# Second feed-forward product: blocks P3 and P7 exchanged, the last norms spread over P7 and P4 without GpSimd

## The chip, the cores and the metric

One core of one Trainium2 chip runs the whole layer in float32. The metric is the device time of one execution in microseconds (us). Three runs of the kernel before gave 1181.56, 1182.09 and 1875.72 us; the median is 1182.09 us. The profiled execution took 1181.23 us, with a span of 1179.4 us from its first to its last instruction.

## The reference

The layer is a mixer (convolution, chunkwise mLSTM, differential attention, an output product), a norm, a feed-forward part and a second norm. Only the end matters here:

```python
x = layer_norm(DEEPNORM_ALPHA * x + h, ln1_g[l], ln1_b[l])
h = jnp.square(jax.nn.relu(x @ w_up[l])) @ w_down[l]
x = layer_norm(DEEPNORM_ALPHA * x + h, ln2_g[l], ln2_b[l])
```

x is 1024 x 1024, w_up 1024 x 4096, w_down 4096 x 1024. `layer_norm` subtracts the mean of each token's 1024 values, divides by the root of the variance plus 1e-5, multiplies by g and adds b.

## The kernel before

The second feed-forward product (hidden 1024 x 4096 by w_down 4096 x 1024) is computed with seven block products instead of eight (Strassen's scheme), P1 to P7. Tokens stand in eight tiles ("rows" 0 to 7, 128 tokens each), output columns in two halves of 512. Every operand is split into a rounded part `hi` (a cast on ACT) and a rest `lo` (a subtraction on DVE), so each product is three matmuls: hi hi, lo hi, hi lo.

The product runs in two passes (c = 0 and 1, half of the hidden units each), a pass in seven blocks of GC = 4 steps, a step in 24 matmuls of 128x512. One table sets the order of the blocks; the table of the first product, `ORDER`, serves both. `down_prep(n)` loads the hidden tile of step n (`hraw`), casts and subtracts; it is called AHEAD = 3 steps early. The weight block of step n is B11, B21, B22 or a sum T1 to T4. Tiles live in 47 slots that are handed out in the order in which they were given back.

A block accumulates in four PSUM banks, one for a token tile: P1, P6, P7, P4 in one set (`abank`), P2, P5, P3 in the other (`bbank`); P1, P2 and P5 start on new banks, the others add on top of what stands there. After a block `gather` adds its banks to the accumulators `accs[row]` on DVE, one instruction of 128x512 for each bank. So P1, P2 feed columns 0 of rows 0 to 3, P6 and P3 their columns 1, P5 and P7 columns 1 of rows 4 to 7, P4 their columns 0. Rows 0 to 3 are complete after P3, rows 4 to 7 after P4. In the second pass P4 runs row by row (4 x 24 matmuls), and the norm of a row follows its gather.

`last_norm` takes statistics with two BN_STATS of 512 columns and one BN_AGGR on DVE, the inverse root as Ln and Exp on ACT with one Newton step on DVE, and applies them one row later: columns 0 on ACT (scale and bias), then DVE (gain) and GpSimd (bias), columns 1 in two DVE instructions. Row 6 has its gain on GpSimd too; row 7 runs on DVE alone, its output in four pieces. All transfers are issued on SP's queue.

The instructions of an engine stand in the order in which a scheduler put them by priority when the program was built; an engine works them off in that order, and one that waits holds up those behind it.

Of the kernel before, what the change touches and what calls it, by code (L numbers as in the profile page):

```python
# [31 lines left out]
EPS = 1e-5  # L32
# [65 lines left out]
def mixer_block(ctx: ExitStack, tc: tile.TileContext, a: dict, out: bass.AP):  # L98
    nc = tc.nc
    const = ctx.enter_context(tc.tile_pool(name="const", bufs=1))  # L100
    spool = ctx.enter_context(tc.tile_pool(name="slots", bufs=1))
    small = ctx.enter_context(tc.tile_pool(name="small", bufs=2))
# [6 lines left out]
    act, dve = nc.scalar, nc.vector  # L109
# [7 lines left out]
    def load(out, in_):  # L117
        nc.sync.dma_start(out=out, in_=in_)
# [19 lines left out]
    epsc = const.tile([P, 1], F32, name="epsc")  # L138
# [32 lines left out]
    css = [slice(half * 512, half * 512 + 512) for half in range(2)]  # L171
# [619 lines left out]
        load(b[:, :D], a[name + "_b"].to_broadcast([P, D]))  # L791
        return g, b

    def stats(z, full=True, n=2):

        st = small.tile([P, n, 6], F32, tag=f"bst{n}", name="bst", bufs=4 // n)
        for i in range(n):
            dve.bn_stats(out=st[:, i, :], in_=z[:, i * (D // n):(i + 1) * (D // n)])  # L798
        mv = small.tile([P, 5], F32, name="bmv")
        dve.bn_aggr(out=mv[:, 0:2], in_=st)  # L800
        act.activation(mv[:, 2:3], mv[:, 1:2], AF.Ln, bias=epsc)
        act.activation(mv[:, 2:3], mv[:, 2:3], AF.Exp, scale=-0.5)

        dve.tensor_scalar(out=mv[:, 1:2], in0=mv[:, 1:2], scalar1=EPS, scalar2=None, op0=ALU.add)
        dve.scalar_tensor_tensor(out=mv[:, 3:4], in0=mv[:, 2:3], scalar=mv[:, 1:2],
                                 in1=mv[:, 2:3], op0=ALU.mult, op1=ALU.mult)
        dve.scalar_tensor_tensor(out=mv[:, 2:3], in0=mv[:, 3:4], scalar=3.0, in1=mv[:, 2:3],  # L807
                                 op0=ALU.subtract, op1=ALU.mult)
        if full:
            dve.tensor_scalar(out=mv[:, 2:3], in0=mv[:, 2:3], scalar1=-0.5, scalar2=None,  # L810
                              op0=ALU.mult)
        return mv


# [2 lines left out]
    b0, b1, b2 = (ml_qk(b) for b in range(3))  # L817
# [94 lines left out]
    F = Slots(spool, [])  # L912
# [39 lines left out]
    def add(out, p, q):  # L952
        dve.tensor_tensor(out=out, in0=p, in1=q, op=ALU.add)  # L953
# [8 lines left out]
    ORDER = ("P1", "P2", "P6", "P5", "P7", "P3", "P4")  # L962
# [192 lines left out]


    GC = NS // 4
    NSTEP = 2 * 7 * GC
    wd, ops_d = {}, {}

    def wd_load(c, g, names):
        s0 = 2 * (GC * c + g)
        for nme in names:
            i, j = int(nme[1]) - 1, int(nme[2]) - 1
            t = F.alloc(F32, nme)
            load(t[:, :1024].rearrange("p (s n) -> p s n", s=2),
                 a["w_down"][NS * i + s0:NS * i + s0 + 2, :, 512 * j:512 * j + 512]
                 .rearrange("s p n -> p s n"))
            wd[c, g, nme] = t
# [22 lines left out]

    def step_of(n):
        c, r = divmod(n, 7 * GC)
        return c, ORDER[r // GC], r % GC

    def down_prep(n):
        c, p, g = step_of(n)
        n_ = slice(0, 1024)
        raw = F.alloc(F32, "hraw")  # L1200
        load(raw[:, n_].rearrange("p (s n) -> p s n", s=2), hdram[GC * c + g][:, HOF[p], :, :])
        keep = c == 0 and BOF[p] in ("B11", "B21")
        ops_d[n] = (*halves_of(raw),
                    *halves_of(wd[c, g, BOF[p]] if keep else wd.pop((c, g, BOF[p])), keep))
# [17 lines left out]
    accs, seen = {}, set()  # L1222
# [9 lines left out]
    def acc_load(rows):  # L1232
        for tb in rows:
# [3 lines left out]
    TO = dict(P1=((0, 0),), P2=((0, 0),), P6=((0, 1),), P5=((4, 1),), P7=((4, 1),), P3=((0, 1),),  # L1237
              P4=((4, 0),))

    def last_norm(tb):  # L1240

        z = accs[tb][:, :D]
        mv = stats(z, False, 2)
        mu, w = mv[:, 0:1], mv[:, 2:3]

        def apply():
            if tb == TB - 1:
                for cs in css:
                    dve.scalar_tensor_tensor(out=z[:, cs], in0=z[:, cs], scalar=mu, in1=g2[:, cs],
                                             op0=ALU.subtract, op1=ALU.mult)  # L1250
                for i in range(4):
                    cs = slice(i * 256, i * 256 + 256)
                    dve.scalar_tensor_tensor(out=z[:, cs], in0=z[:, cs], scalar=w, in1=b2[:, cs],
                                             op0=ALU.mult, op1=ALU.add)
                    load(out[tb * P:tb * P + P, cs], z[:, cs])
                return
            za, zb = z[:, css[0]], z[:, css[1]]
            dve.scalar_tensor_tensor(out=mv[:, 4:5], in0=mu, scalar=-1.0, in1=w, op0=ALU.mult,
                                     op1=ALU.mult)
            act.activation(za, za, AF.Identity, scale=w, bias=mv[:, 4:5])  # L1260
            dve.scalar_tensor_tensor(out=zb, in0=zb, scalar=mu, in1=g2[:, css[1]],
                                     op0=ALU.subtract, op1=ALU.mult)
            mul = nc.gpsimd if tb == TB - 2 else dve
            mul.tensor_tensor(out=za, in0=za, in1=g2[:, css[0]], op=ALU.mult)
            nc.gpsimd.tensor_tensor(out=za, in0=za, in1=b2[:, css[0]], op=ALU.add)
            dve.scalar_tensor_tensor(out=zb, in0=zb, scalar=w, in1=b2[:, css[1]], op0=ALU.mult,  # L1266
                                     op1=ALU.add)
            load(out[tb * P:tb * P + P, css[1]], zb)
            load(out[tb * P:tb * P + P, css[0]], za)

        late.append(apply)
        while len(late) > (0 if tb == TB - 1 else 1):
            late.popleft()()

    late = deque()


    with lane(6):
# [77 lines left out]
    g2 = b2 = None  # L1356
    for n in range(NSTEP):
        c, p, g = step_of(n)
        k = n % (7 * GC)
        final = c == 1 and p == "P4"  # L1360
        if c == 0 and k < GC:
            wd_load(0, k, ("B12",))
        if c == 0 and 2 <= k < 2 + GC:
            wd_load(0, k - 2, ("B22",))
        if n + AHEAD < NSTEP:
            down_prep(n + AHEAD)
        if g == 0:
            if p in ("P1", "P2", "P5"):
                banks = [bank() for _ in range(4)]
                if p == "P1":  # L1370
                    abank[:] = banks
                else:
                    bbank[:] = banks
        if not final:
            down_mm(n, range(4), g == 0, g == GC - 1)
            F.free(*ops_d.pop(n))
        elif g == GC - 1:
            for tb in range(4):
                for m in range(n - GC + 1, n + 1):
# [123 lines left out]
```

## Time and profile before

| | us |
|---|---|
| median of the runs shown | 1182.09 |
| profiled execution | 1181.23 |
| its span | 1179.4 |
| PE busy in the span | 1135.5 (96%) |
| DVE busy | 848.3 (72%) |
| ACT busy | 558.8 (47%) |
| POOL (GpSimd) busy | 13.8 (1%) |

A row of the timeline shows start, duration, engine, line, operation, output and inputs of an instruction; "x4" merges equal ones that follow each other, and what stands in brackets is idle time before it and what ended it. A row of a table by stretch shows, for each engine, busy time and number of instructions, then the granted TensorE clock (1.00 is 2.4 GHz), the busy share of the DMA engines and GB/s. Each duration is that of one instruction; neighbours on an engine overlap a little.

### The profile page before, as it was taken

To read this page: it belongs to the slowest core of one execution; us is meant where nothing else is said; L and a number is where in the kernel's file an instruction comes from. 1 tells how busy PE (TensorE), PEld (TensorE's weight loads), DVE (VectorE), ACT (ScalarE), POOL (GpSimd) and SP (SyncE) were. 2 spreads that over 40 slices of the span, in tenths; PEclk is the share of its full clock that TensorE was granted. 3 is DMA by queue.
4 is the path that set the end of the run, shared out by engine and by line. 5 is a ranking of instruction groups with operands and counts; after the bars stand their busy time and mean duration, and the time that the engine had idled before them with its cause. 6 is when DMAs were issued, how large, how long until landed. Compare 5 with 4: busy or idle time off the path is not lost.

```text
span 1179.4 us, 14960 instructions
## 1 busy us (share of the span) xinstructions
PE 1135.5 (96%) x5630; PEld 932.5 (79%) x5630; DVE 848.3 (72%) x1263; ACT 558.8 (47%) x902; POOL 13.8 (1%) x12
## 2 busy tenths in 40 slices
PE   8999999999999999599999999999999999999993
PEld 6898778877887777487888888888888888888882
DVE  5999668864765738789976767655589666766758
ACT  6212483475664628457654444544534323344411
POOL 0000000000000000000000000000000000000013
PEclk9999999999999999799999999999999999999997
DMA  7202135445635671521376464544884545343303
GB/s 278 73 10 72 36 107 155 147 138 155 168 101 177 224 202 59 168 90 60 144 246 244 167 234 170 196 143 152 313 329 171 186 178 170 116 143 125 107 30 113
DMA packets 82648, 179.86 MB, mean 152 GB/s; under 512 B 7760, under 2 KB 29328, under 8 KB 82576
## 3 DMA queue, kind: packets, MB, share of 16 engines
q1 hardware_dynamic: 82576, 178.91, 45.2%
q8 instruction: 44, 0.72, 0.2%
q14 instruction: 28, 0.23, 0.1%
HBM read 120.12 MB, written 58.72 MB: 152 GB/s over the span
## 4 chain that ended last, share of the span: by engine, by line
PE 88%; DVE 6%; DMA 2%; ACT 2%; issue 1%; SPq 0%; DVEq 0%; ACTq 0%
PE f L933 50%; PE mm L112 27%; PE s L112 5%; PE t L112 4%; PE t L115 2%; DMA raw<-in_w_out 1%; DVE bst L798 1%; DVE lo L148 1%; ACT pp L736 1%; DMA vh<-v 0%; DVE bmv L807 0%; DVE nm L734 0%; DVE acc L953 0%; DMA v<-vh 0%; DVE acc L1266 0%
## 5 line engine op out<-in xcount | busy, mean ns | idle before, releaser
L933 PE MATMUL f<-hi,lo 128*128 128x512 f32 x832 | 327.2, 393 | 0.0
L933 PE MATMUL f<-hi 128*128 128x512 f32 x832 | 327.1, 393 | 0.0
L933 PE MATMUL f<-lo,hi 128*128 128x512 f32 x832 | 326.9, 393 | 0.0
L933 PEld LDWEIGHTS f<-hi 128*128 128x128 f32 x832 | 156.6, 188 | 35.7
L933 PEld LDWEIGHTS f<-lo,hi 128*128 128x128 f32 x832 | 156.4, 188 | 35.9
L933 PEld LDWEIGHTS f<-hi,lo 128*128 128x128 f32 x832 | 156.1, 188 | 36.0
L112 PE MATMUL mm<-xh,hi 128*128 128x512 f32 x240 | 95.7, 400 | 5.7 <-ACT xh L147 5.7
L147 ACT CAST hi<-hraw 128x1024 fp32r<-128x1024 f32 x56 | 58.4, 1049 | 89.8 <-DMA hraw<-h 87.6
L148 DVE TENSOR_TENSOR lo<-hraw,hi 128x1024 fp32r<-128x1024 f32 x56 | 68.2, 1222 | 42.7 <-ACT hi L147 39.2
L112 PE MATMUL mm<-xh,lo 128*128 128x512 f32 x240 | 95.9, 400 | 0.0
L112 PE MATMUL mm<-xl,hi 128*128 128x512 f32 x240 | 95.9, 400 | 0.0
L285 DVE SCALAR_TENSOR_TENSOR cacc<-ypad,pc,cacc 128x1024 f32<-128x1024 f32 x60 | 74.2, 1286 | 0.6
L112 PE MATMUL mm<-hi,xh 128*128 128x256 f32 (+1 forms) x256 | 74.0, 289 | 0.0
L112 PE MATMUL mm<-hi,xl 128*128 128x256 f32 (+1 forms) x256 | 73.2, 286 | 0.0
L112 PE MATMUL mm<-lo,xh 128*128 128x256 f32 (+1 forms) x256 | 73.1, 286 | 0.0
L112 PE MATMUL mm<-hi,yh 128*128 128x512 f32 x128 | 52.7, 411 | 10.8 <-ACT yh L147 9.2
L147 ACT CAST hi<-B 128x1024 fp32r<-128x1024 f32 x36 | 37.6, 1049 | 52.0 <-PE f L933 39.3
L736 ACT ACTIVATE pp<-s,nm 128x128 f32<-128x128 f32 (+7 forms) x64 | 47.7, 747 | 27.2 <-DVE nm L734 18.1
L734 DVE TENSOR_REDUCE nm<-s 128x1 f32<-128x128 f32 (+7 forms) x64 | 47.9, 752 | 16.8 <-PE s L112 16.3
L148 DVE TENSOR_TENSOR lo<-B,hi 128x1024 fp32r<-128x1024 f32 x36 | 43.8, 1221 | 18.7 <-ACT hi L147 13.1
L112 PEld LDWEIGHTS mm<-xh,hi 128*128 128x128 f32 x240 | 45.6, 190 | 14.3 <-ACT xh L147 5.7
L148 DVE TENSOR_TENSOR lo<-raw,hi 128x1024 fp32r<-128x1024 f32 (+3 forms) x34 | 39.3, 1161 | 23.4 <-ACT hi L147 19.6
(264 smaller groups left out, 2046.6 us busy)
## 6 DMA issues: line engine op xcount, KB each, us to landing
hraw<-h SPq DMA_DIRECT2D x56, 512.0 KB, 3.5
w<-in_w_up SPq DMA_DIRECT2D x32, 512.0 KB, 5.4
B<-in_w_down SPq DMA_DIRECT2D x32, 512.0 KB, 4.8
h<-hp SPq DMA_DIRECT2D x16, 512.0 KB
h<-hq SPq DMA_DIRECT2D x16, 512.0 KB, 3.1
h<-hx SPq DMA_DIRECT2D x16, 512.0 KB
raw<-in_wfm SPq DMA_DIRECT2D x14, 512.0 KB, 3.8
qk<-th SPq DMA_DIRECT2D x8, 512.0 KB
```

Source lines behind the costliest of these rows:

```text
L112: return nc.tensor.matmul(out, lhsT=lhsT, rhs=rhs, start=start, stop=stop)
L115: nc.tensor.transpose(out, in_, ident[:k, :k])
L147: act.copy(hi, src)
L148: dve.tensor_tensor(out=lo, in0=src, in1=hi.bitcast(F32), op=ALU.subtract)
L285: dve.scalar_tensor_tensor(out=av, in0=yp[:, i:i + S], scalar=col(PC_DWW + 31 * c + i), in1=av, op0=ALU.mult, op1=ALU.add)
L734: dve.tensor_reduce(out=nm[:, m:m + 1], in_=s_[:, 0:nk], axis=AX.X, op=ALU.max, negate=True)
L736: act.activation(pp[m][:, 0:nk], s_[:, 0:nk], AF.Exp, bias=nm[:, m:m + 1], accum_out=sm[:, m:m + 1])
L798: dve.bn_stats(out=st[:, i, :], in_=z[:, i * (D // n):(i + 1) * (D // n)])
L933: return nc.tensor.matmul(out, lhsT=lhsT, rhs=rhs, start=start and not more, stop=stop and not more, skip_group_check=more)
```

## The change

The second product gets an order of its own, in which P3 comes ahead of P7, in both passes. In the second pass the norms of rows 0 to 3 (`first_norm`) stand beside the four steps of P7: their sums are taken on ACT (one pass of Identity and one of Square, each with an accumulator output into a scrap slot `junk`), and scale and bias are applied to all 1024 columns on ACT, gain and bias on DVE. After P7 `half_stats` takes the BN_STATS of columns 1 of rows 4 to 7, ahead of P4. `last_norm` takes only those of columns 0, and finishes each row at once. No instruction is left on GpSimd; rows 0 to 6 leave in one transfer of 128x1024 each instead of two.

```diff
+    ORDER_D = ("P1", "P2", "P6", "P5", "P3", "P7", "P4")
...
-        return c, ORDER[r // GC], r % GC
+        return c, ORDER_D[r // GC], r % GC
...
+    def newton(mv):
+        dve.scalar_tensor_tensor(out=mv[:, 3:4], in0=mv[:, 2:3], scalar=mv[:, 1:2],
+                                 in1=mv[:, 2:3], op0=ALU.mult, op1=ALU.mult)
+        dve.scalar_tensor_tensor(out=mv[:, 2:3], in0=mv[:, 3:4], scalar=3.0, in1=mv[:, 2:3],
+                                 op0=ALU.subtract, op1=ALU.mult)
+
+    def finish_row(tb, mv):
+        z = accs[tb][:, :D]
+        act.activation(z, z, AF.Identity, scale=mv[:, 2:3], bias=mv[:, 4:5])
+        dve.tensor_tensor(out=z, in0=z, in1=g2[:, :D], op=ALU.mult)
+        add(z, z, b2[:, :D])
+        load(out[tb * P:tb * P + P, :], z)
+
+    def first_norm(tb):
+        z = accs[tb][:, :D]
+        junk = F.alloc(F32, "junk")
+        mv = small.tile([P, 6], F32, tag="mvf", name="mvf")
+        act.activation(junk[:, :D], z, AF.Identity, accum_out=mv[:, 0:1])
+        dve.tensor_scalar(out=mv[:, 5:6], in0=mv[:, 0:1], scalar1=-1.0 / D, scalar2=None,
+                          op0=ALU.mult)
+        act.activation(junk[:, :D], z, AF.Square, bias=mv[:, 5:6], accum_out=mv[:, 1:2])
+        act.activation(mv[:, 2:3], mv[:, 1:2], AF.Ln, scale=1.0 / D, bias=epsc)
+        act.activation(mv[:, 2:3], mv[:, 2:3], AF.Exp, scale=-0.5)
+        dve.tensor_scalar(out=mv[:, 1:2], in0=mv[:, 1:2], scalar1=1.0 / D, scalar2=EPS,
+                          op0=ALU.mult, op1=ALU.add)
+        newton(mv)
+        dve.tensor_tensor(out=mv[:, 4:5], in0=mv[:, 5:6], in1=mv[:, 2:3], op=ALU.mult)
+        F.free(junk)
+        finish_row(tb, mv)
...
+    def half_stats(tb):
+        st = halves[tb] = small.tile([P, 2, 6], F32, tag=f"hst{tb}", name="hst", bufs=1)
+        dve.bn_stats(out=st[:, 1, :], in_=accs[tb][:, css[1]])
+
     def last_norm(tb):
-        z = accs[tb][:, :D]
-        mv = stats(z, False, 2)
+        z, st = accs[tb][:, :D], halves[tb]
+        dve.bn_stats(out=st[:, 0, :], in_=z[:, css[0]])
...
+        act.activation(w, mv[:, 1:2], AF.Ln, bias=epsc)
+        act.activation(w, w, AF.Exp, scale=-0.5)
+        dve.tensor_scalar(out=mv[:, 1:2], in0=mv[:, 1:2], scalar1=EPS, scalar2=None, op0=ALU.add)
+        if tb < TB - 1:
+            newton(mv)
...
+            finish_row(tb, mv)
+            return
...
+        if c == 1 and p == "P7":
+            first_norm(g)
...
-            if c == 1 and p == "P3":
-                for tb in range(4):
-                    last_norm(tb)
+            if c == 1 and p == "P7":
+                for tb in range(4, TB):
+                    half_stats(tb)
```

In the rows that follow, `acc_7562`, `acc_7579`, `acc_7606`, `acc_7631` are rows 0 to 3 and `acc_8016`, `acc_8053`, `acc_8090`, `acc_8131` rows 4 to 7; `f_` are PSUM banks, `mvf_` and `bmv_` the small statistics of a row.

On DVE before, this stands from the gathers of P3 in the second pass on:

```order
L953 TENSOR_TENSOR acc_7562<-acc_7562,f_9200 128x512
L953 TENSOR_TENSOR acc_7579<-acc_7579,f_9201 128x512
L798 BN_STATS bst_9614<-acc_7562 128x6
L953 TENSOR_TENSOR acc_7606<-acc_7606,f_9202 128x512
L953 TENSOR_TENSOR acc_7631<-acc_7631,f_9203 128x512
L800 BN_AGGR bmv_9617<-bst_9614 128x2
```

On DVE now, from the end of row 2's norm to the statistics ahead of P4:

```order
L1250 TENSOR_TENSOR acc_7606<-acc_7606,ln2g_9079 128x1024
L1265 TENSOR_SCALAR mvf_9632<-mvf_9632 128x1
L951 TENSOR_TENSOR acc_7606<-acc_7606,ln2b_9080 128x1024
L1241 SCALAR_TENSOR_TENSOR mvf_9632<-mvf_9632 128x1
L1243 SCALAR_TENSOR_TENSOR mvf_9632<-mvf_9632 128x1
L1268 TENSOR_TENSOR mvf_9632<-mvf_9632 128x1
L951 TENSOR_TENSOR acc_8016<-acc_8016,f_8755 128x512
L1250 TENSOR_TENSOR acc_7631<-acc_7631,ln2g_9079 128x1024
L951 TENSOR_TENSOR acc_8053<-acc_8053,f_8756 128x512
L951 TENSOR_TENSOR acc_7631<-acc_7631,ln2b_9080 128x1024
L951 TENSOR_TENSOR acc_8090<-acc_8090,f_8757 128x512
L951 TENSOR_TENSOR acc_8131<-acc_8131,f_8758 128x512
```

The gathers of P7 (banks f_8755 to f_8758, rows 4 to 7) now stand behind the Newton step of row 3 and the whole of rows 0 to 2; the four BN_STATS of columns 1 come right behind them.

At the end of the program DVE had this, from the gather of row 7 on:

```order
L953 TENSOR_TENSOR acc_8131<-acc_8131,f_8758 128x512
L804 TENSOR_SCALAR bmv_9802<-bmv_9802 128x1
L1264 TENSOR_TENSOR acc_8053<-acc_8053,ln2g_9079 128x512
L805 SCALAR_TENSOR_TENSOR bmv_9802<-bmv_9802 128x1
L1266 SCALAR_TENSOR_TENSOR acc_8053<-acc_8053,bmv_9759,ln2b_9080 128x512
L807 SCALAR_TENSOR_TENSOR bmv_9802<-bmv_9802 128x1
L798 BN_STATS bst_9842<-acc_8131 128x6 x2
L1258 SCALAR_TENSOR_TENSOR bmv_9802<-bmv_9802 128x1
L1261 SCALAR_TENSOR_TENSOR acc_8090<-acc_8090,bmv_9802,ln2g_9079 128x512
L800 BN_AGGR bmv_9845<-bst_9842 128x2
```

and has this now:

```order
L1250 TENSOR_TENSOR acc_8090<-acc_8090,ln2g_9079 128x1024
L951 TENSOR_TENSOR acc_8131<-acc_8131,f_8758 128x512
L951 TENSOR_TENSOR acc_8090<-acc_8090,ln2b_9080 128x1024
L1281 BN_STATS hst_9680<-acc_8131 128x6
L1283 BN_AGGR mvf_9832<-hst_9680 128x2
L1295 SCALAR_TENSOR_TENSOR acc_8131<-acc_8131,mvf_9832,ln2g_9079 128x512
L1287 TENSOR_SCALAR mvf_9832<-mvf_9832 128x1
L1295 SCALAR_TENSOR_TENSOR acc_8131<-acc_8131,mvf_9832,ln2g_9079 128x512
```

Between the gather of row 7 and its aggregate there stood parts of rows 5 and 6; now only one addition of row 6 stands there, and the gather itself stands behind row 6's gain.

On PE in the second pass, where P5 ends and P3 begins (banks f_9200 to f_9203 for both), the first matmul on each bank now waits for a semaphore of DVE; the block that followed P5 before wrote other banks:

```order
L931 MATMUL f_9203<-hi_9196,lo_9193 128x512
L931 MATMUL f_9200<-hi_9234,hi_9230 128x512 [waits DVE_49,Activation_49]
L931 MATMUL f_9200<-lo_9235,hi_9230 128x512
L931 MATMUL f_9200<-hi_9234,lo_9231 128x512
L931 MATMUL f_9201<-hi_9234,hi_9230 128x512 [waits DVE_49]
L931 MATMUL f_9201<-lo_9235,hi_9230 128x512
L931 MATMUL f_9201<-hi_9234,lo_9231 128x512
L931 MATMUL f_9202<-hi_9234,hi_9230 128x512 [waits DVE_49]
```

The same holds from P7 to P4, and for both places in the first pass.

## Rows read from the trace of the kernel before

**Rows 1.** First line of the page: the span.

```profile
span 1179.4 us, 14960 instructions
```

**Rows 2.** Busy time by stretch: P7, P3 and P4 of the second pass.

```profile
1114.47:1136.65 22.18, 22.18 (x97) 18.06 (x96) 8.43 (x10) 4.00 (x4) 0.00 (x0) 1.00 0.00 0
1136.65:1158.80 22.15, 22.15 (x97) 17.95 (x96) 22.15 (x52) 5.50 (x14) 6.77 (x4) 1.00 0.19 72
1158.80:1179.40 20.60, 2.15 (x10) 1.40 (x8) 17.59 (x36) 3.83 (x9) 6.84 (x4) 0.61 0.35 127
```

**Rows 3.** Timeline of DVE: gathers of P5, P7 and P3, then the end.

```profile
1092.29 2.78 DVE L953 TENSOR_TENSOR acc<-acc,f 128x512 f32<-128x512 f32 x4
...
1114.47 1.39 DVE L953 TENSOR_TENSOR acc<-acc,f 128x512 f32<-128x512 f32 x2 [0.85 <-PE f L933]
...
1136.65 1.37 DVE L953 TENSOR_TENSOR acc<-acc,f 128x512 f32<-128x512 f32 x2 [12.28 <-PE f L933]
...
1151.59 1.26 DVE L807 SCALAR_TENSOR_TENSOR bmv<-bmv 128x1 f32<-128x1 f32 x1
...
1171.17 1.69 DVE L1249 SCALAR_TENSOR_TENSOR acc<-acc,bmv,ln2g 128x512 f32<-128x512 f32 x1
...
1174.76 1.67 DVE L1253 SCALAR_TENSOR_TENSOR acc<-acc,bmv,ln2b 128x256 f32<-128x256 f32 x4
```

**Rows 4.** Groups of DVE from 1130 us on: busy, mean ns, idle before.

```profile
L798 DVE BATCH_NORM_STATS2 bst<-acc 128x6 f32<-128x512 f32 x14 | 9.1, 672 | 0.0
L807 DVE SCALAR_TENSOR_TENSOR bmv<-bmv 128x1 f32<-128x1 f32 x8 | 5.6, 698 | 0.0
...
L805 DVE SCALAR_TENSOR_TENSOR bmv<-bmv 128x1 f32<-128x1 f32 x8 | 3.0, 380 | 0.0
```

**Rows 5.** Timeline of POOL: one of its eight instructions.

```profile
1151.01 1.83 POOL L1265 TENSOR_TENSOR acc<-acc,ln2b 128x512 f32<-128x512 f32 x1 [2.14 <-issue]
```

**Rows 6.** Groups of ACT over the whole span, columns as before.

```profile
L147 ACT CAST hi<-hraw 128x1024 fp32r<-128x1024 f32 x56 | 58.4, 1049 | 89.8 <-DMA hraw<-h 87.6 <-PE f L933 1.8 <-DVE lo L148 0.3
...
L1128 ACT ACTIVATE hq<-hq 128x1024 f32<-128x1024 f32 x16 | 17.0, 1060 | 0.4
...
L736 ACT ACTIVATION_READ_ACCUMULATOR pp<-s,nm 128x1 f32 x64 | 12.9, 202 | 0.0
...
L903 ACT ACTIVATE acc<-acc,bmv 128x1024 f32<-128x1024 f32 x8 | 9.8, 1242 | 6.0 <-DVE bmv L901 5.9
```

**Rows 7.** Timeline of DVE in the first norm, around one row's aggregate.

```profile
538.40 0.19 DVE L800 BATCH_NORM_AGGREGATE bmv<-bst 128x2 f32<-128x12 f32 x1
```

**Rows 8.** Timeline of ACT for that row: Exp, then the scaling.

```profile
538.95 0.20 ACT L802 ACTIVATE bmv<-bmv 128x1 f32<-128x1 f32 x1
...
540.15 2.37 ACT L903 ACTIVATE acc<-acc,bmv 128x1024 f32<-128x1024 f32 x2
```

**Rows 9.** Timeline of DVE: gathers of P5 in the first pass; two splits in a row.

```profile
937.52 1.39 DVE L1230 SCALAR_TENSOR_TENSOR acc<-acc,f 128x512 f32<-128x512 f32 x2 [1.41 <-PE f L933]
939.41 1.23 DVE L148 TENSOR_TENSOR lo<-hraw,hi 128x1024 fp32r<-128x1024 f32 x1 [0.50 <-ACT hi L147]
940.56 1.28 DVE L1230 SCALAR_TENSOR_TENSOR acc<-acc,f 128x512 f32<-128x512 f32 x2
...
1061.12 2.36 DVE L148 TENSOR_TENSOR lo<-hraw,hi 128x1024 fp32r<-128x1024 f32 x2 [2.36 <-ACT hi L147]
```

**Rows 10.** Timeline of ACT: two of the last casts of the second pass.

```profile
1114.37 1.05 ACT L147 CAST hi<-hraw 128x1024 fp32r<-128x1024 f32 x1 [2.00 <-DMA hraw<-h]
...
1122.07 1.05 ACT L147 CAST hi<-T 128x1024 fp32r<-128x1024 f32 x1 [3.73 <-PE f L933]
```

**Rows 11.** Transfers of the page: KB each, median us from issue to landing.

```profile
hraw<-h SPq DMA_DIRECT2D x56, 512.0 KB, 3.5
```

**Rows 12.** Busy time by stretch, where PE waited ahead of the output product.

```profile
490.00:495.00 5.00, 0.07 (x1) 0.07 (x1) 2.03 (x5) 1.02 (x2) 0.00 (x0) 0.50 0.21 62
495.00:500.00 5.00, 5.00 (x12) 3.98 (x13) 1.26 (x3) 0.00 (x0) 0.00 (x0) 0.50 0.01 3
```

More of the change, by code (lines that the diff above doesn't have):

```diff
@@ L792, in gain_bias, with stats @@
         return g, b
-    def stats(z, full=True, n=2):
+    def stats(z, n=2):
         st = small.tile([P, n, 6], F32, tag=f"bst{n}", name="bst", bufs=4 // n)
@@ L808, in stats @@
                                  op0=ALU.subtract, op1=ALU.mult)
-        if full:
-            dve.tensor_scalar(out=mv[:, 2:3], in0=mv[:, 2:3], scalar1=-0.5, scalar2=None,
-                              op0=ALU.mult)
+        dve.tensor_scalar(out=mv[:, 2:3], in0=mv[:, 2:3], scalar1=-0.5, scalar2=None, op0=ALU.mult)
         return mv
@@ L1240, in last_norm @@
+    halves = {}
+    def half_stats(tb):
+        st = halves[tb] = small.tile([P, 2, 6], F32, tag=f"hst{tb}", name="hst", bufs=1)
+        dve.bn_stats(out=st[:, 1, :], in_=accs[tb][:, css[1]])
     def last_norm(tb):
-        z = accs[tb][:, :D]
-        mv = stats(z, False, 2)
+        z, st = accs[tb][:, :D], halves[tb]
+        dve.bn_stats(out=st[:, 0, :], in_=z[:, css[0]])
+        mv = small.tile([P, 6], F32, tag="mvf", name="mvf")
+        dve.bn_aggr(out=mv[:, 0:2], in_=st)
         mu, w = mv[:, 0:1], mv[:, 2:3]
[L1246 to L1257, printed above, removed]
+        act.activation(w, mv[:, 1:2], AF.Ln, bias=epsc)
[3 more added lines that the diff above has]
+            newton(mv)
@@ L1258, in apply @@
             dve.scalar_tensor_tensor(out=mv[:, 4:5], in0=mu, scalar=-1.0, in1=w, op0=ALU.mult,
                                      op1=ALU.mult)
-            act.activation(za, za, AF.Identity, scale=w, bias=mv[:, 4:5])
-            dve.scalar_tensor_tensor(out=zb, in0=zb, scalar=mu, in1=g2[:, css[1]],
+            finish_row(tb, mv)
+            return
+        for cs in css:
+            dve.scalar_tensor_tensor(out=z[:, cs], in0=z[:, cs], scalar=mu, in1=g2[:, cs],
                                      op0=ALU.subtract, op1=ALU.mult)
-            mul = nc.gpsimd if tb == TB - 2 else dve
@@ L1264, in apply @@
[L1264 to L1273, printed above, removed]
@@ L1275, in mixer_block @@
-    late = deque()
+        newton(mv)
+        for i in range(4):
+            cs = slice(i * 256, i * 256 + 256)
+            dve.scalar_tensor_tensor(out=z[:, cs], in0=z[:, cs], scalar=w, in1=b2[:, cs],
+                                     op0=ALU.mult, op1=ALU.add)
+            load(out[tb * P:tb * P + P, cs], z[:, cs])
     with lane(6):
```

## The prediction

> **What bounds the kernel now.** I read the stretches first. The span is 1179.4 us [rows 1]; up to P4 of the second pass PE works without a gap at a granted clock of 1.00, and its last matmul ends at 1158.80 + 2.15 = 1160.95 [rows 2]. Behind it lie 18.4 us without TensorE. The timeline of DVE says what they are: the gathers of P3 start at 1136.65 after 12.28 us in which DVE had nothing to do, and from there to 1174.76 + 1.67 = 1176.43 it never pauses [rows 3]; in P4's 22.15 us DVE is busy for all 22.15 [rows 2], and none of its groups there has idle time before it [rows 4]. So PE sets the time until 1161, and then DVE's backlog of eight row norms does; the last transfers take 1179.4 - 1176.43 = 2.97 us more. In the block before, P3, DVE was busy for 8.43 of 22.18 us and ACT for 4.00 [rows 2]: there is room, but rows 0 to 3 were not complete. At most the 18.4 us behind PE can be won as long as PE's own work stays: 1.6%, less than the 2% (23.6 us) that a measurement of this kernel can tell from no change.
>
> Part of the backlog is blocking. A Newton instruction on one column takes 698 ns in the mean [rows 4]; the one that starts at 1151.59 lasts 1.26 us and ends at 1152.85, where a GpSimd instruction on the same slots ends at 1151.01 + 1.83 = 1152.84 [rows 3, 5]. Undisturbed, four such small instructions and their waits fit between the end of Exp and the scaling, 539.15 to 540.15 [rows 8]: 0.25 us each. Eight at L807 lose 8 x 0.45 = 3.6, eight at L805 8 x 0.13 = 1.0, and one of 512 columns takes 1.69 against about 0.67 for others, 1.0 [rows 3, 4]. That is 5.6 us of pure wait on the engine that sets the end.
>
> **The exchange.** The same seven blocks run with the same loads, casts and subtractions; only P3's and P7's come in the other order. PE has no more matmuls. What it adds is waits at four places: P3 now follows P5 on the same banks, and P4 follows P7. A bank must be gathered before the next block adds to it. A block is 96 matmuls in 22.18 us, 0.231 each [rows 2]. A bank's last matmul stands nine matmuls, 2.08 us, ahead of the next block's first one on that bank, and a gather takes 0.64 (1.28 for two [rows 9]): gathers that follow each other, as P5's four in the second pass (2.78 from 1092.29 on [rows 3]), are done 1.4 us before their bank is wanted and cost nothing. In the first pass a split stands between the second and third gather: P5's begin at 937.52, when nine matmuls (2.08) are left; P3 begins at 939.6 and wants the third bank 1.39 later, at 940.99; its gather ends 0.64 after 940.56, at 941.2, plus the way to PE and the modelled end: I count **0.55 us** [rows 9]. P7 to P4 of the first pass has the same split between the same gathers, but DVE reaches it earlier; nothing there, 0.55 as the other end.
>
> **Norms of rows 0 to 3 beside P7.** P3 now ends where P7 ended, so the gathers of rows 0 and 1 begin at 1114.47 [rows 3]. Prices: an Identity sum is an ACT pass of 1.06 plus 0.20 for reading the accumulator; a Square sum has a per-partition bias, for which the scaling's 1.24 is the nearest row, plus 0.20 [rows 6]; a plain cast, 1.05, is the lower end for both, and 0.4 more than these sums the upper, which (b) below takes up. Ln and Exp take 0.5 a row (Exp starts 0.55 after the aggregate [rows 7, 8]). ACT's queue then runs: the cast at 1114.37 ends at 1115.4 [rows 10]; two Identity sums, 1117.9; the Squares wait for all four gathers and a split (1114.47 + 2.78 + 1.23, [rows 3, 9]) 1118.5, and end at 1121.4; Ln, Ln, Exp 1122.2; a cast 1123.2; row 0's scaling 1124.5; Exp and row 2's Identity 1126.0. The last cast needs a hidden tile whose slot PE frees at 1122.07 [rows 10] and which lands 3.5 later [rows 11]: 1126.0 with its issue, so no wait; it ends at 1127.0. Row 1's scaling waits for DVE until 1127.3 and ends at 1128.6; then Square, Identity, Ln and Exp, Square, row 2's scaling, Ln and Exp: 1.44 + 1.26 + 0.5 + 1.44 + 1.24 + 0.5 = 6.4, 1135.0. On DVE row 2's gain runs from 1134.6, its bias addition ends 2 x 1.13 later (two instructions of 1024 columns take 2.36, one 1.23 [rows 9]) at 1136.9, row 3's three small ones at 1137.6, and the gather of P7's first bank at 1138.2. P4 begins at 1160.95 - 22.18 - 0.16 (the modelled end) = 1138.6. **PE does not wait, by 0.4 us.** This is the tightest place of the change. The scrap slots give the later tiles slots that came back up to a step later; in this walk only the last cast notices. On SP the outputs stand behind every load, as before, so four transfers that leave earlier hold nothing up, and seven of 512 KB instead of fourteen halves move the same bytes, the last of them 4 us ahead of row 7's.
>
> Behind it on DVE stand row 3's gain and bias, three gathers and the four half statistics: row 3's scaling ends at 1138.9, then 2 x 1.13 + 3 x 0.60 + 4 x 0.60 = 6.5 (0.60 is the step of 512 columns, 672 ns in the mean less the overlap [rows 4]): 1145.4. P4's first row is complete on PE at 1138.6 + 5.55 = 1144.2, so the rows start 1.2 us late.
>
> **Rows 4 to 7.** A row is now one serial chain: gather 0.60, the addition of the row before 1.13, statistics 0.60, aggregate to scaling 1.75 less one small instruction = 1.50 [rows 7, 8], scaling 1.24, gain 1.13: 6.2 us, against 5.55 that PE takes for a row. DVE falls 0.65 behind with each row. Row 7's gather starts at 1145.4 + 3 x 6.2 = 1164.0. Then 0.60, row 6's addition 1.13, statistics 0.60, aggregate 0.23, two halves 1.4, two small 0.5, four quarters 1.67 [rows 3]: 6.1, 1170.1. Ln and Exp end under the two halves.
>
> **The sum.** 1170.1 + 2.97 + 0.55 = 1173.6 against 1179.4: 5.8 us less. I counted whole durations where neighbours on an engine overlap by about 0.1 (2.36 for two of 1.23): some fifteen such steps from ACT's second half to row 7 on, 1 to 1.5 us, so 7 us less. On the profiled execution's own 1181.23 that is 1174.2; the runs at 1181.56 and 1182.09 stand 0.3 to 0.9 above it, which puts the median at **1175.0**. GpSimd's 13.6 us of work [rows 2] go to DVE and ACT, and are in these chains.
>
> **Rivals.** (a) *A block waits for all four gathers of the last, not for its own bank.* Then P3 and P4 start when the last gather ends. First pass: 941.84 against 939.6, 2.2 us, twice; second pass, P5: 1095.07 against 1094.4, 0.7; P7: by the walk above the fourth gather ends at 1143.0, 4.4 after P4 should begin. 9.5 us in all, 9.0 more than I count: **1184**, slower than before. It decides from 7 us on. For it speaks that all four places are new; against it, that on PE each bank's first matmul has a wait of its own. The Trainium skill (Perfetto Trace Analysis, section Matmuls) says independent groups should rotate through banks so that an eviction overlaps the next group's matmuls; by that rule this exchange is wrong at four places, and (a) is its price; the trace of before has no such place, so it neither agrees nor disagrees. Chance 0.06.
>
> (b) *ACT's sums are dearer, and P4 waits for them.* The gather of P7's first bank stands behind row 3's statistics; each us that ACT is late beyond 0.4 is one of PE. With 0.4 more for each of the eight sums it is 2.8 us: 1178. With twice that, 1181; where PE stood idle ahead of the output product the clock was 0.50 for the idle stretch and for 5 us of work behind it [rows 12], and a long wait here could do the same, 1183. Chance 0.14.
>
> (c) *The chain of a row is shorter than 5.55 us*, and the end follows PE: row 7's gather at 1161, the rest 5.0 to 6.1: 1172. Chance 0.14.
>
> (d) *It does not do what it says:* the norms of rows 0 to 3 slip beside P4 because casts and loads ahead of the sums arrive late, or small DVE instructions stay slow without GpSimd. Half of the gain is lost: 1178.5. Chance 0.08.
>
> **Numbers.** My forecast has 0.58 and spans 1173 to 1177.5. Range: 1171.5 takes in (c) with both small ends; 1179.5 takes in (d) and most of (b); (a) and the rest of (b) stay out. Faster by over 2% would need an end before 1158.5, ahead of PE's last matmul: 0.01. Slower by over 2% is beyond (a) and (b) together: 0.01. Within 2%: 0.98.
>
> **What would show it.** After the change PE's last matmul ends within 1 us of 1161 and no POOL instruction stands in the end; the gathers of rows 0 and 1 still start near 1114.5; P7's first gather starts at 1136.7 to 1137.6 and PE shows no gap ahead of P4; L1243's small instructions take under 0.3 us; DVE ends 7 to 9 us behind PE. Wrong I am if PE has gaps at P3 or P4, if Square with accumulator costs over 1.7, or if DVE's rows keep pace with PE.

## The result, and the profile after

The changed kernel takes **1175.4 us** (median of six runs, 1174.5 to 1177.2; the kernel before beside it 1181.6, five runs from 1179.8 to 1183.9). The ratio on record is 0.9943, 95% interval 0.9932 to 0.9954 (the two medians alone give 0.9948). That is 0.57% less, inside the 2% that count as no change. The forecast was 1175.0, the range 1171.5 to 1179.5. One execution of the kernel before (1875.7 us) and one of e5 below (1871.6 us, the profiled one, at a granted clock of 0.557) were far slower than all others and are left out.

The same three stretches of time as in [rows 2] (span; PE, PEld, DVE, ACT and POOL busy; granted clock, DMA share, GB/s). By the block that PE works on they were P3, P4 and the end before (the heading of [rows 2] names them by the gathers that they begin with) and are P7, P4 and the end now, some 1.6 us later in the changed kernel:

```profile
1114.47:1136.65 22.18, 22.18 (x97) 18.07 (x97) 18.29 (x33) 16.76 (x30) 0.00 (x0) 1.00 0.31 110
1136.65:1158.80 22.15, 22.15 (x97) 17.90 (x96) 16.78 (x33) 4.73 (x7) 0.00 (x0) 1.00 0.18 72
1158.80:1173.40 14.60, 3.83 (x17) 2.75 (x15) 9.57 (x21) 2.24 (x5) 0.00 (x0) 0.77 0.29 108
```

DVE went from 8.43 to 18.29 us in the block ahead of P4, from 22.15 to 16.78 in P4, and the end is 6.0 shorter. PE is busy throughout the first two. The timeline of DVE answers to [rows 3] (start, duration, operation, idle time before and who ended it):

```profile
1116.08 1.37 DVE L951 TENSOR_TENSOR acc<-acc,f 128x512 f32<-128x512 f32 x2 [0.84 <-PE f L931]
...
1138.25 0.69 DVE L951 TENSOR_TENSOR acc<-acc,f 128x512 f32<-128x512 f32 x1 [0.91 <-PE f L931]
...
1141.72 1.28 DVE L951 TENSOR_TENSOR acc<-acc,f 128x512 f32<-128x512 f32 x2
1142.92 2.46 DVE L1277 BATCH_NORM_STATS2 hst<-acc 128x6 f32<-128x512 f32 x4
1145.89 0.69 DVE L951 TENSOR_TENSOR acc<-acc,f 128x512 f32<-128x512 f32 x1 [0.51 <-PE f L931]
...
1164.20 0.68 DVE L951 TENSOR_TENSOR acc<-acc,f 128x512 f32<-128x512 f32 x1
1164.80 1.22 DVE L951 TENSOR_TENSOR acc<-acc,ln2b 128x1024 f32<-128x1024 f32 x1
...
1168.73 1.67 DVE L1300 SCALAR_TENSOR_TENSOR acc<-acc,mvf,ln2b 128x256 f32<-128x256 f32 x4
```

P3's gathers, P7's first gather and row 4's gather all wait for PE: DVE is on time up to there. The gathers of rows 5 to 7 no longer wait; row 7's is shown. PE's last matmul ends at 1162.6, DVE at 1168.73 + 1.67 = 1170.40, 7.8 us later (before 1176.43 - 1160.95 = 15.5 [rows 2, 3]). The chain of waits says why (start, length, engine, tile):

```profile
546.47 388.28 PE f L931 x1680
934.75 4.26 DMA hraw<-h
939.08 1.05 ACT hi L147
942.04 203.82 PE f L931 x882
1146.61 0.71 DVE hst L1281
1148.82 1.25 ACT acc L1249
1150.10 1.24 DVE acc L1250
1151.35 1.83 DVE acc L951 x2
1153.21 0.70 DVE hst L1281
1155.43 1.25 ACT acc L1249
...
1164.29 1.73 DVE acc L951 x2
1166.90 0.75 DVE acc L1295
1169.62 0.79 DVE acc L1300 x2
```

PE, then from row 4 on one chain that passes each row from DVE to ACT and back. And at 934.75 there is something that the chain of before does not have: a transfer and a cast at the first pass's change from P5 to P3.

**One measure for all kernels below.** The stages ahead of this product end at other times in each execution: the first gather of the first pass starts at 869.6 to 873.0 us, with no order among the kernels. So I count from that gather to the end of DVE's last instruction in the profiled execution. "P5 to next" is the time from P5's first gather of the first pass to the first gather of the block behind it, "block ahead of P4" the same for the last two blocks of the second pass. Each ratio is against runs of before taken beside that kernel; e9 to e11 ran on another chip than e1 to e8.

| kernel | ratio to before, 95% | first gather to DVE's end | P5 to next | block ahead of P4 |
|---|---|---|---|---|
| before | 1 | 1176.43 - 870.80 = 305.63 | 22.02 | 22.18 |
| changed | 0.9943, 0.9932 to 0.9954 | 1170.40 - 871.75 = 298.65 | 22.49 | 22.17 |
| e1, GpSimd's work left out | 0.9928, 0.9915 to 0.9940 | 298.39 | 22.01 | 22.18 |
| e2, GpSimd's work on DVE | 0.9972, 0.9960 to 0.9984 | 302.92 | 22.01 | 22.18 |
| e3, exchange alone | 0.9926, 0.9914 to 0.9938 | 296.47 | 22.91 | 23.31 |
| e4, no exchange | 0.9971, 0.9959 to 0.9983 | 302.56 | 22.01 | 22.18 |
| e5, Identity sums twice | 0.9939, 0.9923 to 0.9955 | - | - | - |
| e6, no half statistics | 0.9939, 0.9925 to 0.9953 | 299.09 | 22.90 | 22.17 |
| e7, no ACT in the row's chain | 0.9924, 0.9906 to 0.9941 | 296.68 | 23.10 | 22.17 |
| e8, e7 and second pass only | 0.9903, 0.9886 to 0.9921 | 295.38 | 22.01 | 22.15 |
| e9, sums on DVE | 0.9952, 0.9940 to 0.9964 | 300.26 | 23.71 | 23.54 |
| e10, e3 and second pass only | 0.9903, 0.9890 to 0.9916 | 295.56 | 22.01 | 23.32 |
| e11, all sums twice | 0.9938, 0.9924 to 0.9951 | 298.90 | 23.08 | 22.17 |

The changed kernel has 6.98 us less in this measure. It is one execution of each kernel. How well it repeats can be seen from e6, in which DVE has the same 253 instructions in the same order from that gather on as in the changed kernel: it lies 0.44 higher, and 0.41 of that stand at "P5 to next".

### The profile page after: what moved, and what is told of

Its sections match the earlier page's. It is cut to its first block, busy times and chain, and to the rows that moved or that the text cites. A ratio compares the mean times of both kernels' runs of the same rounds, so it can differ in the third digit from the quotient of the medians.

```text
span 1173.4 us, 14923 instructions
## 1 busy us (share of the span) xinstructions
PE 1136.4 (97%) x5630; PEld 933.1 (80%) x5630; DVE 842.6 (72%) x1249; ACT 570.1 (49%) x918; POOL 0.2 (0%) x4
## 4 chain that ended last, share of the span: by engine, by line
PE 87%; DVE 5%; DMA 4%; ACT 3%; issue 1%; SPq 0%; DVEq 0%; ACTq 0%
PE f L931 50%; PE mm L112 25%; PE s L112 5%; PE t L112 3%; PE t L115 2%; DMA kh<-qk 1%; DVE lo L148 1%; DMA raw<-in_w_out 1%; ACT pp L736 1%; DVE acc L951 1%; DMA vh<-v 1%; DVE nm L734 0%; ACT wth L147 0%; DMA hraw<-h 0%; DVE pp L742 0%
```

## The experiments

### What GpSimd cost before (e1, e2)

```diff
-            mul = nc.gpsimd if tb == TB - 2 else dve
-            mul.tensor_tensor(out=za, in0=za, in1=g2[:, css[0]], op=ALU.mult)
-            nc.gpsimd.tensor_tensor(out=za, in0=za, in1=b2[:, css[0]], op=ALU.add)
+            if tb < TB - 2:                                    # e1
+                dve.tensor_tensor(out=za, in0=za, in1=g2[:, css[0]], op=ALU.mult)
+            dve.tensor_tensor(..., g2 ...); dve.tensor_tensor(..., b2 ...)   # e2
```

> The kernel before with its eight GpSimd instructions left out (the bias addition on columns 0 to 511 of rows 0 to 6 and row 6's gain there; the output lacks them). DVE's own instructions stay as they are. My theory (GpSimd holds back the small DVE instructions): the eight at L807 and their neighbours fall to 0.15 to 0.22 us each. The mean durations gave 5.6 us of blocking; read one by one in the timeline they are 7.4 (L805 0.4, L1258 0.65, four L807 of 1.1, L1249 0.95, L805 1.0), of which 0.6 comes back because row 7's gather then waits for PE: 1175 us. Rival (the small instructions wait for ACT or for the row before, GpSimd is only a neighbour): they stay near 1.2 us and the time stays at 1182.

> The kernel before with the same eight instructions on DVE in place of GpSimd, nothing left out. My theory: DVE takes 8 x 0.60 = 4.8 us more work and loses 7.4 of blocking: 1179 us, so 2.5 to 3 us faster than before. Rival (no blocking): 4.8 more, 1186.6.

Measured: 1173.5 and 1179.0 us. The timeline of DVE in e1, where [rows 3] had 1.26 and 1.69:

```profile
1151.62 0.15 DVE L807 SCALAR_TENSOR_TENSOR bmv<-bmv 128x1 f32<-128x1 f32 x1
...
1166.96 0.74 DVE L1249 SCALAR_TENSOR_TENSOR acc<-acc,bmv,ln2g 128x512 f32<-128x512 f32 x1
...
1168.60 1.67 DVE L1253 SCALAR_TENSOR_TENSOR acc<-acc,bmv,ln2b 128x256 f32<-128x256 f32 x4
```

Nothing but GpSimd's instructions is gone, DVE does not pause at the end in either kernel, and its own instructions are short now: 305.63 - 298.39 = 7.2 us of blocking, not the 5.6 that I had worked out from means. With the work on DVE 2.7 us of it remain (302.92); 7.2 less 8 x 0.60 would be 2.4. The rival is refuted.

### The exchange and the norms apart (e3, e4)

```diff
+    ORDER_D = ("P1", "P2", "P6", "P5", "P3", "P7", "P4")   # e3: before, with this order
...
+        if c == 1 and p == "P7":
+            last_norm(g)                                   # as before, GpSimd included
...
-    ORDER_D = ("P1", "P2", "P6", "P5", "P3", "P7", "P4")   # e4: changed kernel, old order
+    ORDER_D = ORDER
...
-        if c == 1 and p == "P7":
-            first_norm(g)
...
+            if c == 1 and p == "P3":
+                for tb in range(4): first_norm(tb)
```

> The kernel before with P3 and P7 exchanged and the norms of rows 0 to 3 beside P7, but each norm as it was: statistics on DVE, bias additions on GpSimd, both statistics of rows 4 to 7 in P4. My theory (the exchange wins time only until PE's own pace binds): rows 4 to 7 take 5.2 us of DVE each, less than PE's 5.55, so row 7's gather starts at about 1163 in place of 1165.2, and the 11.2 us from there to DVE's end stay, blocking included: 2 to 3 us less than before, 1179. Rival (the exchange carries all of the gain): 1175.5. Rival (nothing gained without the sums on ACT, because DVE is then late for P4): 1182.

> The changed kernel with the old order of the blocks: norms of rows 0 to 3 (sums on ACT) stand beside P4, the half statistics of rows 4 to 7 beside P3. My theory (the exchange is what makes room; the new norms alone are serial chains): four rows of about 4.1 us on ACT from 1137.3 on, row 3 done at about 1156, then rows 4 to 7 at 6.2 each: DVE ends at about 1180, 1185 us (1182 to 1189), slower than before. Rival (the norms' new form and the missing GpSimd work carry the gain): 1176 or less.

Measured: 1173.8 and 1178.4. **Both expectations were wrong.** The exchange alone wins more (9.2 us in the measure) than the whole change (7.0), the norms alone win 3.1. In e3 GpSimd has the same eight instructions as before; POOL's timeline at one instruction beside P7 and one in P4:

```profile
1135.27 1.83 POOL L1266 TENSOR_TENSOR acc<-acc,ln2b 128x512 f32<-128x512 f32 x1 [2.76 <-issue]
...
1152.33 1.29 POOL L1266 TENSOR_TENSOR acc<-acc,ln2b 128x512 f32<-128x512 f32 x1 [10.51 <-DVE acc L1265]
```

and DVE's at the same places:

```profile
1135.19 0.74 DVE L1267 SCALAR_TENSOR_TENSOR acc<-acc,bmv,ln2b 128x512 f32<-128x512 f32 x1
1135.85 1.27 DVE L807 SCALAR_TENSOR_TENSOR bmv<-bmv 128x1 f32<-128x1 f32 x1
...
1152.48 0.69 DVE L953 TENSOR_TENSOR acc<-acc,f 128x512 f32<-128x512 f32 x1 [0.29 <-PE f L933]
1153.20 1.29 DVE L798 BATCH_NORM_STATS2 bst<-acc 128x6 f32<-128x512 f32 x2
...
1163.57 0.69 DVE L953 TENSOR_TENSOR acc<-acc,f 128x512 f32<-128x512 f32 x1 [1.20 <-PE f L933]
...
1167.10 1.67 DVE L1254 SCALAR_TENSOR_TENSOR acc<-acc,bmv,ln2b 128x256 f32<-128x256 f32 x4
```

Beside P7 a small instruction is held until GpSimd's ends (1135.27 + 1.83 = 1137.10, 1135.85 + 1.27 = 1137.12), and GpSimd's itself had started beside a DVE instruction of 512 columns with two operands in SBUF (1135.19). In P4 GpSimd's stands beside a gather, whose second operand is in a bank, and statistics, which read one operand: the gather keeps its 0.69 and the two statistics their 1.29, and GpSimd itself needs 1.29 instead of 1.83. DVE waits for PE ahead of each row there, so the row before has come to GpSimd by the time of the gather. I had taken the blocking for a property of the instructions; it depends on what DVE runs beside them. The Trainium skill (SBUF — State Buffer, section "Who interferes with whom") says that a DVE instruction with two SBUF inputs contends with a GpSimd one that reads SBUF, that one with at most one SBUF input, outside the modes that use both ports, does not, and that the pair of ports over which they contend is locked by one of the two; these rows agree (held until 1137.12, or 0.69 and 1.29 as elsewhere).

In e4 I had walked the rows of P4 one after the other. The built program takes them in pairs, as the timeline of DVE shows:

```profile
1144.20 2.35 DVE L1250 TENSOR_TENSOR acc<-acc,ln2g 128x1024 f32<-128x1024 f32 x2
1146.47 2.35 DVE L951 TENSOR_TENSOR acc<-acc,ln2b 128x1024 f32<-128x1024 f32 x2
...
1171.46 1.22 DVE L951 TENSOR_TENSOR acc<-acc,ln2b 128x1024 f32<-128x1024 f32 x1
```

so one row's ACT time lies beside another's DVE time, and DVE ends at 1172.7 instead of 1180.

### Are ACT's sums tight, do the half statistics matter (e5, e6)?

```diff
         act.activation(junk[:, :D], z, AF.Identity, accum_out=mv[:, 0:1])
+        act.activation(junk[:, :D], z, AF.Identity, accum_out=mv[:, 0:1])    # e5
...
-        dve.bn_stats(out=st[:, 1, :], in_=accs[tb][:, css[1]])               # e6: from half_stats
...
-        dve.bn_stats(out=st[:, 0, :], in_=z[:, css[0]])
+        for i in range(2): dve.bn_stats(out=st[:, i, :], in_=z[:, css[i]])   # e6: to last_norm
```

> The changed kernel with each Identity sum of rows 0 to 3 taken twice: four ACT passes of 1.05 + 0.18 more. My theory (ACT's queue beside P7 carries rows 0 to 3, and P4 waits behind row 3): 4.9 us more, less 0.9 in which ACT waited for a transfer anyway, so 4.0 at row 3's small instructions; P7's first gather, which stood 0.9 us early, starts 3.1 late, PE stands idle 3.1 ahead of P4, and everything behind it moves: 1178.5 us (up to 1181 if the clock falls). Rival (the end is DVE's, 7.8 us behind PE, so ACT's delay disappears in it): 1175.4.

> The changed kernel with both statistics of rows 4 to 7 in P4, none ahead. My theory (a row is one serial chain on DVE and ACT): row 4 still starts when PE has its bank, rows 4 to 7 then take 0.6 more each: 2.4 us, 1177.8. Rival (the half statistics only fill time in which DVE waits for PE): 1175.4.

Measured: 1175.2 and 1174.9, no difference from the changed kernel in either: the rivals' numbers, not mine. e5 has no trace to read beside the others, only its times. e6 tests nothing: its four early statistics stand at the same place in the trace as in the changed kernel (1144.62, 2.46, x4, behind P7's gathers), so the scheduler put them ahead of the gathers that wait for PE by itself. The explicit call that the change adds is not needed for that; what the statistics would cost in P4 stays open. e5 left open whether the sums have room or the order goes around them; e11 takes that up.

### The row's chain, and the first pass (e7, e8)

```diff
         if tb < TB - 1:
+            dve.scalar_tensor_tensor(out=z, in0=z, scalar=mu, in1=g2[:, :D],
+                                     op0=ALU.subtract, op1=ALU.mult)
             newton(mv)
-            dve.scalar_tensor_tensor(out=mv[:, 4:5], in0=mu, scalar=-1.0, in1=w, ...)
-            finish_row(tb, mv)
+            dve.scalar_tensor_tensor(out=z, in0=z, scalar=w, in1=b2[:, :D],
+                                     op0=ALU.mult, op1=ALU.add)
+            load(out[tb * P:tb * P + P, :], z)
...
-        return c, ORDER_D[r // GC], r % GC
+        return c, (ORDER, ORDER_D)[c][r // GC], r % GC       # e8, with the above
```

> The changed kernel with rows 4 to 6 scaled on DVE in two fused passes over 1024 columns, (z - mean) times gain while ACT has Ln and Exp, then times w plus bias, in place of scaling on ACT, gain and bias. My theory (the serial chain of 6.2 us against PE's 5.55 makes rows 5 to 7 late, ACT's 1.24 and the wait for it are part of it): the chain is about 0.6 + 0.6 + 0.2 + 1.35 + 0.5 + 1.35 = 4.6, each row's gather waits for PE again, row 7's starts at 1163.1 in place of 1164.2 and row 6's addition no longer stands behind it: 2.2 us less, 1173.1. Rival (DVE's work as such sets the end, not the chain): two passes of 1.35 in place of two of 1.14 make it 0.4 a row longer, 1176.5.

> As e7_no_act_in_chain, with P3 and P7 exchanged in the second pass alone. My theory (the exchange costs PE 0.5 to 0.7 us at the first pass's handovers from P5 to P3 and from P7 to P4): 0.6 less than e7, 1172.5, and the end of PE's last matmul, counted from the first matmul of the first pass, 0.5 to 0.7 earlier. Rival (the later end of PE is chance from stages ahead): the same as e7.

Measured: 1172.6 and **1170.2 us**. In e7 row 7's gather waits for PE again, as the timeline of DVE shows, and nothing of row 6 stands behind it:

```profile
1159.11 1.28 DVE L1292 SCALAR_TENSOR_TENSOR acc<-acc,mvf,ln2b 128x1024 f32<-128x1024 f32 x1
1161.11 0.69 DVE L951 TENSOR_TENSOR acc<-acc,f 128x512 f32<-128x512 f32 x1 [0.71 <-PE f L931]
1161.83 0.69 DVE L1281 BATCH_NORM_STATS2 hst<-acc 128x6 f32<-128x512 f32 x1
```

A row takes 1155.51 - 1149.92 = 5.59 us, PE's pace. DVE has 2 x 1.28 of work a row in place of 1.23 + 1.23 and ends earlier: the chain set the end, not the work. 298.65 - 296.68 = 1.97 us, and this execution lost 0.61 more than the changed kernel's at "P5 to next" (23.10 against 22.49); without that it is 2.6, against 2.2 expected. With the old order in the first pass "P5 to next" falls to 22.01, and e8's chain of waits is PE alone from 544.67 us on, long before this product, and then one row:

```profile
544.67 615.43 PE f L931 x2664
1160.13 0.70 DVE acc L951
1160.85 0.70 DVE hst L1281
1161.83 0.75 DVE acc L1297
1164.54 0.79 DVE acc L1302 x2
```

The medians of e7 and e8 are 2.4 apart, where I had expected 0.6, the measure 1.3, the block 1.09; the last is what the exchange cost in the first pass of e7's profiled execution. The rest of the medians' difference stays open: e7's six runs spread from 1171.1 to 1175.9.

### Sums on DVE, old norms, all sums twice (e9 to e11)

```diff
-        act.activation(junk[:, :D], z, AF.Identity, accum_out=mv[:, 0:1])    # e9: in first_norm
+        for i in range(2): dve.bn_stats(out=st[:, i, :], in_=z[:, css[i]])
+        dve.bn_aggr(out=mv[:, 0:2], in_=st)
...
-        return c, ORDER_D[r // GC], r % GC                                   # e10: in e3
+        return c, (ORDER, ORDER_D)[c][r // GC], r % GC
...
+        act.activation(junk[:, :D], z, AF.Identity, accum_out=mv[:, 0:1])    # e11: once more
+        act.activation(junk[:, :D], z, AF.Square, bias=mv[:, 5:6], accum_out=mv[:, 1:2])
```

> The changed kernel with the statistics of rows 0 to 3 on DVE (two instructions of 0.6 and an aggregate a row) in place of the sums on ACT. My theory (the sums are off the path as long as P7's gathers need not wait for them): DVE's 18.3 us beside P7 become some 23.5, 1.3 more than the block has, and DVE is idle for 4.2 us beside P4: 0 to 1 us more than the changed kernel, 1175.4 to 1176.4; from the first pass's first gather to DVE's end 298.7 to 299.7, against 298.65 measured for the changed kernel. Rival (without ACT's sums DVE is late for P4): 1178 or more, and a block P7 of over 24 us.

> As e3_exchange_alone, with P3 and P7 exchanged in the second pass alone: the old norms, GpSimd's additions among them. My theory (from the first pass's first gather to DVE's end e3 took 296.47, of which 0.9 are the first pass's handover from P5 to P3): 295.6, 1171.5 us, within 1 us of e8; GpSimd's instructions cost nothing as long as DVE waits for PE and they run beside gathers and statistics. Rival (e8's norms are what makes it fast): 1173.5 or more.

> The changed kernel with the Identity and the Square sum of rows 0 to 3 both taken twice, 4 x (1.23 + 1.33) = 10.2 us more on ACT. ACT's 16.8 us beside P7 become 27, 4.8 more than the block. My theory after e5 (the order in which P7's gathers and the rows' small instructions stand is made when the kernel is built, and goes around a later ACT): rows 2 and 3 slip into P4, where DVE has 4.2 us to spare, and their gains and additions push rows 5 to 7: 2 to 4 us more, 1177.5 to 1179.5. Rival as I had predicted it (P4 waits behind row 3): 8 us more, 1183.

Measured: 1177.8, 1171.9 and 1176.2. e10 came out as worked out (295.56 against 295.6): with the exchange in the second pass alone the old norms, GpSimd and all, are as fast as e8.

e9's 300.26 lies 1.6 above the changed kernel, 0.6 above the range that I had given. P7's gathers are 1.37 late, but PE's waits from 850 us on (total, times, longest) show 0.2 for them and 1.4 for the first pass, where nothing was edited:

```profile
PE f L931 <- DVE acc L1229: 1.4, 1, 1.4
PE f L931 <- DVE acc L951: 0.2, 1, 0.2
```

Moving the sums to DVE therefore costs some 0.4 us: row 4's gather comes 30.19 behind P3's first (1148.55 - 1118.36) in place of 29.81 (1145.89 - 1116.08). The rest is a transfer; the timelines of SP, ACT and DVE of e9 at the first pass's P5:

```profile
935.88 0.34 SPq L118 DMA_DIRECT2D hraw<-h  x1
...
941.43 2.00 ACT L147 CAST hi<-hraw 128x1024 fp32r<-128x1024 f32 x2 [4.50 <-PE f L931]
...
939.61 1.39 DVE L1229 SCALAR_TENSOR_TENSOR acc<-acc,f 128x512 f32<-128x512 f32 x2 [1.41 <-PE f L931]
942.51 1.23 DVE L148 TENSOR_TENSOR lo<-hraw,hi 128x1024 fp32r<-128x1024 f32 x1 [1.52 <-ACT hi L147]
943.66 1.28 DVE L1229 SCALAR_TENSOR_TENSOR acc<-acc,f 128x512 f32<-128x512 f32 x2
```

The cast starts 1.82 us behind P5's first gather (941.43 - 939.61), in the changed kernel 0.61 (939.08 - 938.47): 1.21 of the 1.22 between 23.71 and 22.49. Its row names PE, but the last piece of its transfer lands at 941.36, just ahead of it.

e11 fell short of both expectations: 10 us more on ACT cost 0.25 in the measure, with 0.59 more than the changed kernel at "P5 to next", so nothing behind it. Its P7 gathers come on time (22.17), and rows 2 and 3 are finished in P4, as I had thought; but there each row's gain now stands behind the next row's gather:

```profile
1153.33 0.69 DVE L951 TENSOR_TENSOR acc<-acc,f 128x512 f32<-128x512 f32 x1 [0.26 <-PE f L931]
1154.05 0.69 DVE L1283 BATCH_NORM_STATS2 hst<-acc 128x6 f32<-128x512 f32 x1
1154.66 1.21 DVE L1250 TENSOR_TENSOR acc<-acc,ln2g 128x1024 f32<-128x1024 f32 x1
```

The gain at 1154.66 is row 4's, behind row 5's gather and statistics: the other order breaks up the chain, and that this gives back what the later rows 0 to 3 cost is how I read it; no run takes the two apart.

## Why the prediction was right, point by point

- **The bound and the size.** -5.8 from the walk, 1 to 1.5 for overlaps, 7 in all; 6.98 in the measure. The profiled executions themselves are 6.03 apart (1181.23 and 1175.20), since the first gather stood 0.95 us later in the changed kernel's; the stages ahead vary between runs. From P3's first gather to DVE's end it is 54.32 us (1170.40 - 1116.08) against 55.63 in the walk (1170.1 - 1114.47): 1.3 less, what I had taken off as a lump. That the handover, the other term, came out near 0.55 is in part luck, as the next point shows. The blocking that I had put at 5.6 was 7.2, but it does not enter the sum.
- **Handover 0.55 from P5 to P3.** 22.49 - 22.02 = 0.47 in the profiled run: the size fits, the working does not. I had taken the third gather's place, 3.04 us behind the first (940.56 - 937.52 [rows 9]), as fixed; it stands behind a split, the split waits for a cast, the cast for a transfer (the DMA row in the chain above). In the changed kernel it stood 2.84 behind; in e3, e6, e7, e9 and e11 the same instructions stood 3.21, 3.24, 3.39, 4.05 and 3.42 behind and cost 0.89, 0.88, 1.08, 1.69 and 1.06. The cost is the delay less 2.31 to 2.37 in all six; with the 3.04 of before it would have been 0.7. In the old order delays of 2.44 (e1) to 3.40 (e2) cost nothing. The term should have been 0.5 to 1.7 with the transfer as its cause. From P7 to P4 in the first pass it is 22.42 from gather to gather, against 22.22 before and 22.29 to 22.60 in e1, e2, e4, e8 and e10, which keep the old order there: nothing, as I had counted.
- **Norms beside P7.** The prices were a little high (timeline of ACT; predicted 1.06 + 0.20 and 1.24 + 0.20):

```profile
1117.44 1.05 ACT L1259 ACTIVATE junk<-acc 128x1024 f32<-128x1024 f32 x1
1118.40 0.18 ACT L1259 ACTIVATION_READ_ACCUMULATOR junk<-acc 128x1 f32 x1
...
1120.09 1.15 ACT L1262 ACTIVATE junk<-acc,mvf 128x1024 f32<-128x1024 f32 x1 [0.46 <-DVE mvf L1260]
1121.15 0.18 ACT L1262 ACTIVATION_READ_ACCUMULATOR junk<-acc,mvf 128x1 f32 x1
```

  PE did not wait. I had called this the tightest place, with 0.4 to spare; it has more. DVE was through with row 3's small instructions 23.1 us behind P3's first gather in my walk (1137.6 - 1114.47) and stood idle there for the last 0.91 of 22.17 us when it ran, so it was 1.9 earlier and the place has some 2.3. From start to start an Identity sum takes 1.05 (1117.44 to 1118.49) and a Square 1.15 (1120.09 to 1121.24), where I had counted 1.26 and 1.44: 2.0 over the eight sums. The half statistics end 29.30 behind P3's first gather (1145.38 - 1116.08); I had 1145.4 - 1114.47 = 30.93. These 1.6 us are part of what I took off as a lump, and so row 4's gather does not start 1.2 us late but waits 0.51 for PE.
- **Rows 4 to 7.** 6.2 a row predicted, (1164.20 - 1145.89) / 3 = 6.10 measured, one serial chain, DVE falling behind. e7 confirms that the chain sets the end. From row 7's gather on 6.20 against 6.1, closing 3.0 against 2.97.
- **Rivals.** (a) Whole groups: in the chain above PE runs unbroken for 203.82 us from 942.04 to row 4's bank, through P3 and P7 of the second pass. That row takes 5.55, so P4 began at about 1140.3, and the fourth of P7's gathers ended at 1141.72 + 1.28 = 1143.00. (a) is out. (b) Dearer sums: the price was wrong in kind. I let each us of ACT beyond 0.4 pass to PE; e11 made the sums 10 us dearer and nothing came through: in the order that was built for it P7's first gather stands ahead of the Newton steps of rows 2 and 3, not behind row 3's. A sum that is dearer on the chip than the scheduler assumes could not be tried this way. (c) did not come about, though e7 and e8 make it so (5.59 a row). (d) The small instructions take 0.14 to 0.22 us, none slow.
- **The signs.** DVE ended 7.8 us behind PE, L1243 took 0.16 and no POOL instruction was left, as said. Two signs in absolute times missed: PE's last matmul ended at 1162.6, 1.7 behind 1160.95 and not within 1, and the gathers of rows 0 and 1 started at 1116.08 and not near 1114.5. Of that 0.95 come from the stages ahead and 0.47 from the handover.
- **What I did not see:** that the exchange alone wins 9.2 us, more than the whole change's 7.0. With it DVE waits for PE in each row of P4, and the cost of GpSimd is gone there without moving its work; the new norms put scaling, gain and bias of a whole row into one chain and give 2.2 back. The ratios' intervals touch (0.9914 to 0.9938 and 0.9932 to 0.9954), so this rests on the measure, where the difference is far above e6's. The parts do not add up: without GpSimd's work the old order, too, is 7.2 better (e1).

## What to carry to other kernels

When an engine falls behind in the last stage, first look for a stage before it with room that can be fed by another order of the blocks; then write the last stage so that a row's chain, not its work, stays under the pace of the engine that feeds it: two fused DVE passes (1.28 us each) beat ACT's 1.25, gain 1.23 and bias 1.23 with two changes of engine between them. Where the old norms keep that pace, they need no rewriting: e10 has e8's ratio. Exchange blocks only in the pass where it is needed: e8 takes 1170.2 us, 0.9903 of before (0.9886 to 0.9921), and that interval lies below the changed kernel's, each against before. Price a new handover by the slowest thing that stands between its gathers, transfers included.

## What the runs showed of the hardware

Beside a GpSimd addition of 512 columns in e3, a gather of DVE with one of its operands in a bank took 0.69 us and two statistics with one operand 1.29, as elsewhere. A DVE instruction with both operands in SBUF was held until GpSimd's ended: one of a single column took 1.27 in place of 0.15, one of 512 columns 1.69 [rows 3] in place of 0.74. GpSimd's own took 1.29 beside the gather and 1.83 where a DVE instruction of 512 columns with both operands in SBUF had started 0.08 us ahead of it (1135.19 and 1135.27).

The transfer of a hidden tile at the first pass's P5, the same instructions in six kernels with the exchange there, moved the handover by 0.5 to 1.7 us from one profiled execution to the next.
